# Two transformer blocks in f32 on one core: a new opening, four gate groups as triples, one mask instruction for two, softmax rows scaled on ScalarE

## The chip, the core and the metric

The kernel runs on one core of a Trainium2 chip. The core has TensorE (PE, matrix products into PSUM), VectorE (DVE), ScalarE (ACT), GpSimd (POOL) and SyncE (SP), which here only issues transfers. Each engine runs its own instructions in order and waits for others by semaphores. The metric is the device time of one execution in microseconds; less is better.

## The reference

Two blocks follow each other on x of 256 tokens by 2048 features. What the change touches is in this cut:

```python
c_act = jax.nn.silu(c)
mod = c_act @ w_ada[l] + b_ada[l]                    # 6 x 2048 values: shifts, scales, gates
sh1, sc1, gt1, sh2, sc2, gt2 = jnp.split(mod, 6, axis=-1)
h = modulate(rms_norm(x, g_mix[l]), sh1, sc1)        # h * (1 + sc1) + sh1
z = h @ w_in[l]
(q_sb, k_sb, v_sb, q_ds, k_ds, v_ds, q_ix, k_ix, w_ix, gate_sb, gate_ds) = split_columns(z)
o_sb = stick_breaking_attention(...)                 # strictly causal, 8 heads of 128
o_ds = indexer_sparse_attention(...)                 # top-k keys by an indexer, softmax, 8 heads
merged = (jax.nn.sigmoid(gate_sb) * (o_sb @ w_o_sb[l])
          + jax.nn.sigmoid(gate_ds) * (o_ds @ w_o_dsa[l]))
x = x + gt1[:, None, :] * (merged @ w_out[l])
...
```

After it come a gated feed-forward of width 5632, and the second block: a norm, a mixer with 8 "nsa" heads (two softmaxes each) and 8 "fox" heads (one softmax each), and a second feed-forward.

## The kernel before

**Products.** x lies transposed in SBUF: 16 k-tiles of 128 features by 256 tokens. A weight is cast to a short f32 (`wh`, on ACT, line 298) and its rest is kept beside it (`wl`, weight minus `wh`, on DVE, line 305; the very first `wl` is made on POOL, line 303). Activations are kept as such a pair too (hi and lo). A product of one 128x128 weight tile with one k-tile is made on PE in one of two forms in `mm_f`. As a *triple*: `wh` x hi, `wh` x lo, `wl` x hi, three matmuls of 256 columns into the same 256 columns of PSUM (lines 349 to 351). As a *pair* (`pair=True`): `wh` times hi and lo side by side, 512 columns, and `wl` x hi, 256 columns (lines 343 to 347); the two halves of PSUM are summed at the end by `gather` (lines 454 and 455): a copy of the first half by ACT, then an add of the second by DVE.

**Order of the work.** `items` is a list, written by hand, of weight blocks of 512 KB (`w`), of blocks of the transposed `w_ada` (`ada`), and of calls. SP loads them in this order into ten (later six) raw buffers; a buffer is free again when DVE has read it (`wl`, or the ada reduction). `run` goes through the groups of products and, ahead of each block, has the casts and the `wl` of the blocks up to three ahead issued (`AHEAD`), the cast one step before the `wl` (`LAG`). An ada item is one DVE reduction of 128x1024 (line 313) with the silu of c, spread over all partitions (`cb`); it gives half of a column of `mod`. Attention heads, norms and the like are generators; `tick`, called after every 1.27 us of PE columns, moves each one step on.

**The opening.** SP loads c, the vectors, x in four transfers and then the raw blocks. PE spreads c over the partitions in four matmuls of 512 columns with one row (line 540), ACT makes their silu into `cb` (line 541), and then four squares of x (line 551). DVE adds them in three steps (lines 554 and 555), and four f32 matmuls with ones sum over the partitions (line 558). `first_norm` (line 560), a call behind the second ada item, takes the reciprocal root: one ACT step, the table of Ln and Exp, Ln, Exp, and four POOL steps (567 to 570) into `rb`. Six ada items on, `h_scale(0)` multiplies the first two k-tiles by `rb` on DVE (line 583), two ada items later `first_h` applies `gain` and `mod` (592 to 605), and products begin. The further k-tiles are scaled on POOL by `h_scale`, in six parts of 2, 2, 3, 3, 3 and 3 k-tiles (`KG`); in each part all columns of `w_in` but the gates get their share over the part's k-tiles.

**Behind the parts.** Stick-breaking heads (`sb_head`, line 633) run beside the last part: two multiplies by the mask `strict` of the blocks on the diagonal, in `nk` and again in `a` (lines 649, 650, 663, 664). Then 32 gate tiles in eight groups of four (`ggs`, line 1031, all pairs); the first four groups (gate_sb) run beside the indexer and its top-k search on DVE. The evacuation of a gate tile is `gate_tile` (line 1001). In softmax heads (`ds_head` 851, `nsa_head` 1544, `fox_head` 1626) `softmax` takes the row maximum on DVE and the exponential with its row sum on ACT; DVE takes the reciprocal, and `scale_rows` (line 840) multiplies the two blocks of rows, 128x128 and 128x256, by it on DVE. `transpose_p` (848) needs the result on PE. `rsqrt_of` (line 492) is the reciprocal root used elsewhere: Ln and Exp on ACT and five DVE steps. PSUM holds four buffers `pg` for products and four `pm` (`psm`) for all else and for every second group of the first five parts.

Of the kernel before, what the change touches and what calls it, by code (L numbers as in the profile page):

```python
# [28 lines left out]
LATE_SMALL = (3, 2)  # L29
OFFS = (1, 2, 1.5, 1, 1, 1)  # L30
FS = (0.8, 0.8, 0.8, 0.8, 0.8, 0.8)
FIRSTS = 1
LESS = 2
RL = (0.75, 0.6)
MORE = 12
# [4 lines left out]
LAND = 45  # L40

FILL = (7, 20)
KG = (2, 2, 3, 3, 3, 3)
KG0 = tuple(sum(KG[:j]) for j in range(len(KG)))

# [78 lines left out]
def kernel(ctx: ExitStack, tc: tile.TileContext, t):  # L124
# [40 lines left out]
    def slot(dt=F32):  # L165
        return ring.tile([128, 8, T], dt, name="ring", tag="ring")
# [24 lines left out]
    def psm():  # L191
        return pm.tile([128, 512], F32, name="pm", tag="pm")

    tables = [None]

    def lut(func, **kw):

        if func in (AF.Exp, AF.Ln) and tables[0] != "ln_exp":
            nc.scalar.add_instruction(mybir.InstLoadActFuncSet(
                name=nc.get_next_instruction_name(), act_func_set_id=LN_EXP, engine=mybir.EngineType.Activation,  # L200
                ins=[], outs=[]))
            tables[0] = "ln_exp"
        elif func not in (AF.Exp, AF.Ln):
            tables[0] = func
        nc.scalar.activation(func=func, **kw)  # L205

# [41 lines left out]
    def call_item(fn):  # L248
        items.append(("call", fn))
# [37 lines left out]
    def split(idx, g, ks, off, stage):  # L287

        it, r = items[idx], raw_of[idx]
        k0, n = ks[0], len(ks)  # L290
        if it[0] == "w":
            w = g.width
            src = r[:, k0 - it[2]:k0 - it[2] + n, off:off + w]
            view = lambda x: x[:, :n * w].rearrange("p (k w) -> p k w", w=w)
            if stage == 0:
                hi = view(wp.tile([128, 1024], F32R, name="wh", tag="wh"))
                half_of[idx, g, k0] = hi
                nc.scalar.activation(out=hi, in_=src, func=AF.Copy)  # L298
            else:
                hi, lo = half_of[idx, g, k0], view(wq.tile([128, 1024], F32R, name="wl", tag="wl"))  # L300
                if state["firsts"]:
                    state["firsts"] -= 1
                    nc.gpsimd.tensor_tensor(out=lo, in0=src, in1=hi.bitcast(F32), op=OP.subtract)
                else:
                    nc.vector.tensor_sub(out=lo, in0=src, in1=hi.bitcast(F32))  # L305
                half_of[idx, g, k0] = (hi, lo)
            return
        if stage == 0:
            return

        c, half = ADA[it[1]][0] + it[2] // 2, it[2] % 2
        below = mod[:, c:c + 1] if half else V["b_ada"][:, c:c + 1]
        nc.vector.tensor_tensor_reduce(out=r, in0=r, in1=P["cb"][:, RAW * half:RAW * half + RAW], scale=1.0,  # L313
                                       scalar=below, op0=OP.mult, op1=OP.add, accum_out=mod[:, c:c + 1])
        if half:
            ada_done.add(c)
# [49 lines left out]
            if last:  # L366
                g.evac(b, g.ps[b])

    state = {"load": 0, "split": [0, 0], "raws": 10, "n": 0, "firsts": FIRSTS}
    AHEAD = (3, 3)  # L370
    LAG = 1

# [162 lines left out]
    nc.vector.memset(onec, 1.0)  # L535
    nc.vector.memset(halfc, 1.5)
    nc.vector.memset(invp, 1.0 / 128)
    for u in range(4):
        ps = psm()
        nc.tensor.matmul(ps, ones[0:1, :], P["cb"][0:1, 512 * u:512 * u + 512], start=True, stop=True)  # L540
        lut(out=P["cb"][:, 512 * u:512 * u + 512], in_=ps, func=AF.Silu)
    cdram = dram.tile([1, D], F32, name="cdram")
    nc.scalar.dma_start(out=cdram, in_=P["cb"][0:1, :])

    sqs = []

    def first_squares():
        sqs.extend([slot(), slot()])
        for j in range(4):
            u = slice(4 * (j % 2), 4 * (j % 2) + 4)  # L550
            nc.scalar.activation(out=sqs[j // 2][:, u, :], in_=xt[j // 2][:, u, :], func=AF.Square)
            if j % 2:
                s = sqs[j // 2]
                nc.vector.tensor_add(out=s[:, 0:4, :], in0=s[:, 0:4, :], in1=s[:, 4:8, :])
        nc.vector.tensor_add(out=sqs[0][:, 0:4, :], in0=sqs[0][:, 0:4, :], in1=sqs[1][:, 0:4, :])
        sqs.append(psm())
        for k in range(4):
            nc.tensor.matmul(sqs[2][:, :T], ones, sqs[0][:, k, :], start=(k == 0), stop=(k == 3))

    def first_norm():  # L560
        ss = sqs[2][:, :T]
        m = tmp.tile([128, T], F32, name="mm", tag="mm", bufs=1)
        r0 = tmp.tile([128, T], F32, name="r0", tag="r0", bufs=1)
        nc.scalar.activation(out=m, in_=ss, func=AF.Identity, scale=1.0 / D, bias=epsc)
        lut(out=r0, in_=m, func=AF.Ln)
        lut(out=r0, in_=r0, func=AF.Exp, scale=-0.5)
        nc.gpsimd.tensor_tensor(out=m, in0=m, in1=r0, op=OP.mult)
        nc.gpsimd.tensor_tensor(out=m, in0=m, in1=r0, op=OP.mult)
        nc.gpsimd.tensor_scalar(out=m, in0=m, scalar1=-0.5, scalar2=1.5, op0=OP.mult, op1=OP.add)
        nc.gpsimd.tensor_tensor(out=rb, in0=r0, in1=m, op=OP.mult)  # L570

    def h_segs(j):
        k0, n = KG0[j], KG[j]
# [3 lines left out]
            k0, n = k0 + m, n - m  # L577

    def h_scale(j):
        eng = nc.gpsimd if j else nc.vector  # L580
        for _, b, u, m in h_segs(j):
            x = xt[b][:, u, :]
            eng.tensor_tensor(out=x, in0=x, in1=rb[:, None, :].to_broadcast([128, m, T]), op=OP.mult)
# [49 lines left out]
    def sb_head(h):  # L633
        q, k, v = bufs["q_sb"], bufs["k_sb"], bufs["v_sb"]
        S = psm()
        nc.tensor.matmul(S[:, 0:256], k[:, h, 0:128], q[:, h, :], start=True, stop=True)
        nc.tensor.matmul(S[:, 256:384], k[:, h, 128:256], q[:, h, 128:256], start=True, stop=True)
        yield
        e = P["ax"].tile([128, 384], F32, name="t0", tag="t0")
        l = P["ax"].tile([128, 384], F32, name="t1", tag="t1")  # L640
        lb = P["ax"].tile([128, 384], F32, name="t2", tag="t2")
        nc.scalar.activation(out=e, in_=S[:, :384], func=AF.Abs)
        lut(out=e, in_=e, func=AF.Exp, scale=-1.0)
        lut(out=l, in_=e, func=AF.Ln, bias=onec)
        yield
        nk = P["ax"].tile([128, 384], F32, name="t3", tag="t3")
        nc.vector.scalar_tensor_tensor(out=nk, in0=S[:, :384], scalar=0.0, in1=l, op0=OP.max, op1=OP.add)
        nc.vector.scalar_tensor_tensor(out=lb, in0=S[:, :384], scalar=0.0, in1=l, op0=OP.min, op1=OP.subtract)
        for o in (0, 256):
            nc.vector.tensor_mul(out=nk[:, o:o + 128], in0=nk[:, o:o + 128], in1=C["strict"])  # L650
        yield from wait(W)
        sf = psm()
        nc.tensor.matmul(sf[:, 0:128], C["sufneg"], nk[:, 0:128], start=True, stop=True)
        nc.tensor.matmul(sf[:, 128:256], C["sufneg"], nk[:, 128:256], start=True, stop=False)
        nc.tensor.matmul(sf[:, 128:256], negones, nk[:, 256:384], start=False, stop=True)
        nc.tensor.matmul(sf[:, 256:384], C["sufneg"], nk[:, 256:384], start=True, stop=True)
        yield
        nc.vector.tensor_add(out=lb, in0=sf[:, :384], in1=lb)
        yield
        a = P["ax"].tile([128, 384], F32, name="t4", tag="t4")  # L660
        lut(out=a, in_=lb, func=AF.Exp)
        yield
        for o in (0, 256):
            nc.vector.tensor_mul(out=a[:, o:o + 128], in0=a[:, o:o + 128], in1=C["strict"])
        yield from wait(W)
        yield from av_out(a, [(v, 128 * h)], need_pair("o_sb"), h)

# [171 lines left out]

    def scale_rows(p, r):  # L840
        for b, (o, n) in enumerate(BLK):
            nc.vector.tensor_scalar(out=p[:, o:o + n], in0=p[:, o:o + n], scalar1=r[:, b:b + 1], scalar2=None,  # L842
                                    op0=OP.mult)

    def transpose_p(p):
        PT = psm()
# [98 lines left out]
        gens["h", 0] = None  # L945

    a0 = ada_items(NKG) + ada_items(0)
    items.extend(a0[:2])
    call_item(first_norm)
    items.extend(a0[2:-2])  # L950
    call_item(lambda: h_scale(0))
    items.extend(a0[-2:])
    call_item(first_h)
    extra = [x for a in range(2 * NKG, 2 * NKG + 2) for x in ada_items(a)]
    more = [0] * (NKG - 1) + [MORE]
# [45 lines left out]
    def gate_tile(which, i):  # L1001
        def evac(ps):
            if i % 8 == 0:
                gates[which, i // 8] = slot()
            gather(gates[which, i // 8][:, i % 8, :], ps)
        return evac

    def ds_chain():
# [19 lines left out]
    add_group(k7)  # L1028
    gl = [(t["w_in"], G_SB + 128 * i, gate_tile(0, i)) for i in range(16)]
    gl += [(t["w_in"], G_DS + 128 * i, gate_tile(1, i)) for i in range(16)]  # L1030
    ggs = f_groups(gl, 16, h_act1, idr, pair=True)
    for u, g in enumerate(ggs[:4]):
        if u == 1:
            g.pre = lambda: drain([gens["sb"]])
# [697 lines left out]

    assert not (ada_rest or ada_late or ada_last), (ada_rest, ada_late, ada_last)
    pump_loads(-1)
    first_squares()
    run()
    while active:
        tick()
# [34 lines left out]
```

## Time and profile before

| | |
|---|---|
| time, median of three runs | 2752.37 us (2750.64 to 2767.28) |
| the profiled execution's own time | 2754.54 us |
| its span, first instruction to last | 2751.9 us |
| granted TensorE clock in it, mean | 0.995 |
| instructions | 42323 |

All rows that the prediction uses are from that one execution. Times in rows count from the start of the span. In a row of the timeline the first number is the start, the second the time until the end of the last of the merged instructions; in brackets stands the idle time of the engine before it and what ended it. In a row of a group, `xN` is the count, then come busy time and the mean of one in ns, then idle time before them. A matmul's end is modelled, so its steps are read from the starts. The f32 matmuls (lines 540 and 558) appear as two instructions each.

### The profile page before, as it was taken

What the parts mean: (1) busy time and instruction counts of PE and PEld (TensorE: products, weight loads), DVE (VectorE), ACT (ScalarE), POOL (GpSimd) and SP (SyncE); (2) the same over time, 40 slices, a digit from 0 to 9 for tenths busy, and PEclk for the clock granted to TensorE, in tenths of its full rate; (3) what the DMA queues carried; (4) which work ended last, traced back from release to release, by engine and by line L of the source; (5) the groups of instructions that cost most, each with busy time, mean ns of one, the idle gap of its engine ahead of it and who ended that gap; (6) DMA issues with size and microseconds to landing.
All of it is one profiled execution on the core that took longest, in us unless ns stands there. A gap on an engine that the chain in (4) does not pass through costs nothing. (4 is left out here: it accounts for less than half of the span.)

```text
span 2751.9 us, 42323 instructions
## 1 busy us (share of the span) xinstructions
PE 2671.3 (97%) x15985; PEld 2339.2 (85%) x15985; DVE 1980.9 (72%) x2881; ACT 1364.6 (50%) x2067; POOL 544.9 (20%) x506
## 2 busy tenths in 40 slices
PE   6899999899999999999999999999999999999999
PEld 5788897798987888888888878888888888888888
DVE  7999986998877886556666756677876665566655
ACT  4555563354536555435554535555554454345543
POOL 1655530220612010000111301102222210012210
PEclk9999999999999999999999999999999999999999
DMA  9888767889985886566666675544566666666664
GB/s 324 261 270 265 259 214 201 279 276 331 310 274 157 302 311 194 189 190 188 184 190 200 186 222 150 161 130 146 176 184 192 195 190 191 190 191 191 188 197 143
DMA packets 302045, 591.16 MB, mean 215 GB/s; under 512 B 20997, under 2 KB 60781, under 8 KB 301711
## 3 DMA queue, kind: packets, MB, share of 16 engines
q1 hardware_dynamic: 298214, 583.61, 66.1%
q10 hardware_dynamic: 3626, 4.85, 0.8%
q8 instruction: 125, 2.05, 0.3%
q14 instruction: 80, 0.65, 0.1%
HBM read 582.54 MB, written 5.78 MB: 214 GB/s over the span
## 5 line engine op out<-in xcount | busy, mean ns | idle before, releaser
L347 PE MATMUL pg<-ring,wh 128*128 128x512 f32 x5408 | 1905.0, 394 | 1.1 <-DVE ring L1181 0.9
L305 DVE TENSOR_TENSOR wl<-raw,wh 128x1024 fp32r<-128x1024 f32 (+1 forms) x921 | 1152.0, 1263 | 620.4 <-ACT wh L298 609.9
L346 PE MATMUL pg<-ring,wl 128*128 128x256 f32 x5408 | 1525.4, 282 | 6.5 <-DVE wl L305 4.6
L298 ACT ACTIVATE wh<-raw 128x1024 fp32r<-128x1024 f32 (+2 forms) x922 | 931.5, 1026 | 876.8 <-PE pg L347 652.2
L347 PEld LDWEIGHTS pg<-ring,wh 128*128 128x128 f32 x5408 | 1021.1, 189 | 215.8 <-DVE ring L1181 3.4
L346 PEld LDWEIGHTS pg<-ring,wl 128*128 128x128 f32 x5408 | 1018.8, 188 | 36.1 <-issue 10.3
L481 POOL TENSOR_TENSOR ring<-gy,ring 128x256 fp32r<-128x256 f32 x88 | 110.1, 1262 | 749.5 <-ACT ring L479 749.5
L349 PE MATMUL pg<-ring,wh 128*128 128x256 f32 x652 | 185.6, 285 | 23.6 <-ACT ring L601 13.8
L351 PE MATMUL pg<-ring,wl 128*128 128x256 f32 x652 | 183.9, 282 | 7.4 <-DVE wl L305 7.2
L350 PE MATMUL pg<-ring,wh 128*128 128x256 f32 x652 | 183.4, 281 | 0.0
L343 PE MATMUL pg<-ring,wh 128*128 128x512 f32 x352 | 143.3, 407 | 6.7 <-DVE ring L455 4.7
L349 PEld LDWEIGHTS pg<-ring,wh 128*128 128x128 f32 x652 | 123.6, 190 | 27.6 <-ACT ring L601 14.5
L466 POOL TENSOR_TENSOR ring<-pt,ring 128x256 f32<-128x256 f32 x95 | 110.8, 1174 | 141.5 <-ACT pt L465 141.2
L313 DVE CUSTOM_DVE_ANT_0 raw<-raw,cb,mod 128x1024 f32<-128x1024 f32 x96 | 134.6, 1402 | 1.5 <-DMA raw<-in_w_adaT 1.2
L351 PEld LDWEIGHTS pg<-ring,wl 128*128 128x128 f32 x652 | 123.4, 189 | 10.5 <-DVE wl L305 10.3
L313 DVE CUSTOM_DVE_ANT_0 raw<-raw,cb,vec 128x1024 f32<-128x1024 f32 x96 | 129.0, 1343 | 1.7 <-DMA cb<-cdram 1.6
L350 PEld LDWEIGHTS pg<-ring,wh 128*128 128x128 f32 x652 | 123.5, 189 | 0.8 <-DVE ring L605 0.2
L1247 POOL TENSOR_TENSOR gy<-ga,rb 128x256 f32<-128x256 f32 x44 | 52.5, 1203 | 325.1 <-ACT ga L205 325.1
L344 PE MATMUL pg<-ring,wl 128*128 128x256 f32 x352 | 99.2, 282 | 0.0
L362 PE MATMUL pg<-wh,ring 128*128 128x512 f32 (+3 forms) x236 | 83.5, 354 | 0.0
L364 PE MATMUL pg<-wh,ring 128*128 128x512 f32 (+3 forms) x236 | 79.1, 335 | 0.0
L363 PE MATMUL pg<-wl,ring 128*128 128x512 f32 (+3 forms) x236 | 78.8, 334 | 0.0
(298 smaller groups left out, 2481.3 us busy)
## 6 DMA issues: line engine op xcount, KB each, us to landing
raw<-in_w_in SPq DMA_DIRECT2D x240, 512.0 KB, 4.8
raw<-in_w_adaT SPq DMA_DIRECT2D x192, 512.0 KB, 5.4
raw<-in_w_gate SPq DMA_DIRECT2D x176, 512.0 KB, 4.4
raw<-in_w_up SPq DMA_DIRECT2D x176, 512.0 KB, 3.8
raw<-in_w_down SPq DMA_DIRECT2D x176, 512.0 KB, 4.5
raw<-in_w_out SPq DMA_DIRECT2D x64, 512.0 KB, 5.5
raw<-in_w_o_sb SPq DMA_DIRECT2D x16, 512.0 KB, 5.9
raw<-in_w_o_dsa SPq DMA_DIRECT2D x16, 512.0 KB, 6.4
```

The lines of the kernel that those rows point to most:

```text
L298: nc.scalar.activation(out=hi, in_=src, func=AF.Copy)
L305: nc.vector.tensor_sub(out=lo, in0=src, in1=hi.bitcast(F32))
L313: nc.vector.tensor_tensor_reduce(out=r, in0=r, in1=P["cb"][:, RAW * half:RAW * half + RAW], scale=1.0, scalar=below, op0=OP.mult, op1=OP.a ...
L343: nc.tensor.matmul(g.ps[f], hi[:, fs], both, start=True, stop=False)
L344: nc.tensor.matmul(ps, lo[:, fs], xh, start=False, stop=False)
L346: nc.tensor.matmul(ps, lo[:, fs], xh, start=False, stop=False)
L347: nc.tensor.matmul(g.ps[f], hi[:, fs], both, start=False, stop=stop)
L349: nc.tensor.matmul(ps, hi[:, fs], xh, start=start, stop=False)
L350: nc.tensor.matmul(ps, hi[:, fs], xl, start=False, stop=False)
L351: nc.tensor.matmul(ps, lo[:, fs], xh, start=False, stop=stop)
L466: nc.gpsimd.tensor_tensor(out=y, in0=x, in1=y, op=OP.add)
L481: nc.gpsimd.tensor_tensor(out=lo, in0=src, in1=hi.bitcast(F32), op=OP.subtract)
```

## The change

The opening: a Square of x stands behind each Silu on ACT; DVE adds within each of the two slots, not across them; eight matmuls sum the squares; the table of Ln and Exp is loaded behind the last Square. `first_norm`, now behind the fourth ada item, uses `rsqrt_of` (DVE), issues twelve f32 matmuls of 512 columns whose result nobody reads (`keep_warm`), and calls `h_scale(0)`. The second part's scaling goes from POOL to DVE, and so does the first `wl`. The gate_sb groups become triples and are evacuated by one ACT copy. The two mask multiplies become one instruction over both diagonal blocks. `scale_rows` is done by ACT, as a Copy with a column as its scale.

```diff
-FIRSTS = 1
...
+WARM = 12
...
-    def lut(func, **kw):
-
-        if func in (AF.Exp, AF.Ln) and tables[0] != "ln_exp":
+    def ln_exp():
+        if tables[0] != "ln_exp":
             nc.scalar.add_instruction(mybir.InstLoadActFuncSet(
...
-                if state["firsts"]:
-                    state["firsts"] -= 1
-                    nc.gpsimd.tensor_tensor(out=lo, in0=src, in1=hi.bitcast(F32), op=OP.subtract)
-                else:
-                    nc.vector.tensor_sub(out=lo, in0=src, in1=hi.bitcast(F32))
+                nc.vector.tensor_sub(out=lo, in0=src, in1=hi.bitcast(F32))
...
+    def keep_warm(n):
+
+        ps = psm()
+        for _ in range(n):
+            nc.tensor.matmul(ps, ones, P["cb"][:, :512], start=True, stop=True)
+
+    sqs = [slot(), slot()]
     for u in range(4):
         ps = psm()
         nc.tensor.matmul(ps, ones[0:1, :], P["cb"][0:1, 512 * u:512 * u + 512], start=True, stop=True)
         lut(out=P["cb"][:, 512 * u:512 * u + 512], in_=ps, func=AF.Silu)
+        v = slice(4 * (u % 2), 4 * (u % 2) + 4)
+        nc.scalar.activation(out=sqs[u // 2][:, v, :], in_=xt[u // 2][:, v, :], func=AF.Square)
+        if u % 2:
+            w = sqs[u // 2]
+            nc.vector.tensor_add(out=w[:, 0:4, :], in0=w[:, 0:4, :], in1=w[:, 4:8, :])
     cdram = dram.tile([1, D], F32, name="cdram")
+    sqs.append(psm())
+    for k in range(8):
+        nc.tensor.matmul(sqs[2][:, :T], ones, sqs[k // 4][:, k % 4, :], start=(k == 0), stop=(k == 7))
+    ln_exp()
     nc.scalar.dma_start(out=cdram, in_=P["cb"][0:1, :])
-    sqs = []
-
-    def first_squares():
...
     def first_norm():
...
+        rsqrt_of(rb, sqs[2][:, :T], 1.0 / D, T)
+        keep_warm(WARM)
+        h_scale(0)
...
-        eng = nc.gpsimd if j else nc.vector
+        eng = nc.gpsimd if j > 1 else nc.vector
...
-        for o in (0, 256):
-            nc.vector.tensor_mul(out=nk[:, o:o + 128], in0=nk[:, o:o + 128], in1=C["strict"])
+        ends = lambda x: x.rearrange("p (a b) -> p a b", b=128)[:, 0:3:2, :]
+        strict = C["strict"][:, None, :].to_broadcast([128, 2, 128])
+        nc.vector.tensor_tensor(out=ends(nk), in0=ends(nk), in1=strict, op=OP.mult)
...
-        for o in (0, 256):
-            nc.vector.tensor_mul(out=a[:, o:o + 128], in0=a[:, o:o + 128], in1=C["strict"])
+        nc.vector.tensor_tensor(out=ends(a), in0=ends(a), in1=strict, op=OP.mult)
...
-            nc.vector.tensor_scalar(out=p[:, o:o + n], in0=p[:, o:o + n], scalar1=r[:, b:b + 1], scalar2=None,
-                                    op0=OP.mult)
+            nc.scalar.activation(out=p[:, o:o + n], in_=p[:, o:o + n], func=AF.Copy, scale=r[:, b:b + 1])
...
-    items.extend(a0[:2])
+    items.extend(a0[:4])
     call_item(first_norm)
-    items.extend(a0[2:-2])
-    call_item(lambda: h_scale(0))
-    items.extend(a0[-2:])
+    items.extend(a0[4:])
     call_item(first_h)
...
-            gather(gates[which, i // 8][:, i % 8, :], ps)
+            if which:
+                gather(gates[which, i // 8][:, i % 8, :], ps)
+            else:
+                nc.scalar.activation(out=gates[which, i // 8][:, i % 8, :], in_=ps[:, :T], func=AF.Copy)
...
-    ggs = f_groups(gl, 16, h_act1, idr, pair=True)
+    ggs = f_groups(gl[:16], 16, h_act1, idr) + f_groups(gl[16:], 16, h_act1, idr, pair=True)
...
-    first_squares()
     run()
```

## Rows read from the trace of the kernel before

**Rows 1.** The page's totals: busy time, share of the span and instructions of each engine.

```profile
PE 2671.3 (97%) x15985; PEld 2339.2 (85%) x15985; DVE 1980.9 (72%) x2881; ACT 1364.6 (50%) x2067; POOL 544.9 (20%) x506
```

**Rows 2.** Windows view: stretch, its length, busy us and instructions by engine, PEclk, DMA.

```profile
40.00:50.00 10.00, 10.00 (x83) 9.73 (x82) 10.00 (x17) 6.21 (x10) 0.00 (x0) 1.00 1.00 346
...
60.00:80.00 20.00, 20.00 (x151) 18.81 (x151) 17.67 (x30) 14.21 (x25) 2.22 (x2) 1.00 0.85 270
...
500.00:550.00 50.00, 42.38 (x277) 37.97 (x276) 48.00 (x85) 20.35 (x22) 14.91 (x8) 0.97 0.82 274
```

**Rows 3.** Timeline of the opening: start, us, engine, line, operation.

```profile
2.44 7.16 PE L540 MATMUL pm<-cb,ones 1*128 1x512 f32 x8 [2.44 <-DMA cb<-in_c]
...
3.65 8.42 SPq L268 DMA_DIRECT2D raw<-in_w_adaT  x8
...
10.81 3.89 ACT L551 ACTIVATE ring<-ring 128x1024 f32<-128x1024 f32 x4 [0.58 <-ACT cb L205]
...
17.14 1.28 DVE L313 CUSTOM_DVE_ANT_0 raw<-raw,cb,vec 128x1024 f32<-128x1024 f32 x1
...
17.37 3.75 PE L558 MATMUL pm<-ring,ones 128*128 128x256 f32 x8 [7.77 <-DVE ring L555]
...
21.65 1.28 ACT L199 ACT_TABLE_LOAD   x1
...
27.46 2.34 POOL L303 TENSOR_TENSOR wl<-raw,wh 128x1024 fp32r<-128x1024 f32 x1
27.53 2.81 DVE L583 TENSOR_TENSOR ring<-ring,rb 128x512 f32<-128x512 f32 x1 [2.71 <-POOL rb L570]
...
35.56 1.28 DVE L313 CUSTOM_DVE_ANT_0 raw<-raw,cb,vec 128x1024 f32<-128x1024 f32 x1
35.74 0.42 PE L351 MATMUL pg<-ring,wl 128*128 128x256 f32 x1
...
36.39 0.41 PE L351 MATMUL pg<-ring,wl 128*128 128x256 f32 x1
...
40.54 0.28 PE L351 MATMUL pm<-ring,wl 128*128 128x256 f32 x1
...
42.58 0.28 PE L351 MATMUL pm<-ring,wl 128*128 128x256 f32 x1
```

**Rows 4.** DMA issues in the first 40 us: KB each, median us to landing.

```profile
raw<-in_w_adaT SPq DMA_DIRECT2D x14, 512.0 KB, 8.6
```

**Rows 5.** PE's waits from 80 to 400 us: total us, times, longest.

```profile
PE pg L351 <- DVE wl L305: 7.2, 8, 1.4
```

**Rows 6.** Timeline of PE in the first gate group.

```profile
427.23 0.28 PE L346 MATMUL pg<-ring,wl 128*128 128x256 f32 x1
...
429.31 0.28 PE L346 MATMUL pg<-ring,wl 128*128 128x256 f32 x1
```

**Rows 7.** PE's waits from 480 to 560 us; four adds of `gather` from DVE's timeline.

```profile
PE pg L346 <- DVE wl L305: 3.7, 3, 2.7
...
PE pg L343 <- DVE ring L455: 2.8, 1, 2.8
PE pg L349 <- DVE ring L455: 1.7, 1, 1.7
...
529.34 1.41 DVE L455 TENSOR_TENSOR ring<-pg,ring 128x256 f32<-128x256 f32 x4
```

**Rows 8.** Lines 842, 650 and 1118 (ns min/median/max); ACT's exponentials of softmax rows.

```profile
L842 DVE TENSOR_SCALAR t<-t,st x64: 285/344/1368, 556.9 to 1968.6; 128x128 f32<-128x128 f32 x32, 128x256 f32<-128x256 f32 x32
...
  PE pm L848: 4.8, 4
...
L650 DVE TENSOR_TENSOR t<-t,conA x16: 276/282/837, 356.1 to 420.6; 128x128 f32<-128x128 f32 x16
...
L1118 ACT ACTIVATE ring<-ring,gain x16: 492/495/510, 1486.6 to 1577.2; 128x256 fp32r<-128x256 f32 x16
...
L205 ACT ACTIVATE t<-t,st 128x128 f32<-128x128 f32 x32 | 12.7, 398 | 33.9 <-DVE st L829 25.1 <-DVE st L832 8.6
```

More of the change, by code (lines that the diff above doesn't have):

```diff
@@ L202, in lut @@
             tables[0] = "ln_exp"
-        elif func not in (AF.Exp, AF.Ln):
+    def lut(func, **kw):
+        if func in (AF.Exp, AF.Ln):
+            ln_exp()
+        else:
             tables[0] = func
@@ L367, in mm_t @@
                 g.evac(b, g.ps[b])
-    state = {"load": 0, "split": [0, 0], "raws": 10, "n": 0, "firsts": FIRSTS}
+    state = {"load": 0, "split": [0, 0], "raws": 10, "n": 0}
     AHEAD = (3, 3)
@@ L541 @@
         lut(out=P["cb"][:, 512 * u:512 * u + 512], in_=ps, func=AF.Silu)
+        v = slice(4 * (u % 2), 4 * (u % 2) + 4)
[3 more added lines that the diff above has]
+            nc.vector.tensor_add(out=w[:, 0:4, :], in0=w[:, 0:4, :], in1=w[:, 4:8, :])
     cdram = dram.tile([1, D], F32, name="cdram")
+    sqs.append(psm())
+    for k in range(8):
+        nc.tensor.matmul(sqs[2][:, :T], ones, sqs[k // 4][:, k % 4, :], start=(k == 0), stop=(k == 7))
+    ln_exp()
     nc.scalar.dma_start(out=cdram, in_=P["cb"][0:1, :])
-    sqs = []
-    def first_squares():
[L548 to L558, printed above, removed]
-    def first_norm():
[L561 to L570, printed above, removed]
+    def first_norm():
+        rsqrt_of(rb, sqs[2][:, :T], 1.0 / D, T)
+        keep_warm(WARM)
+        h_scale(0)
     def h_segs(j):
@@ L1004, in evac @@
                 gates[which, i // 8] = slot()
-            gather(gates[which, i // 8][:, i % 8, :], ps)
+            if which:
+                gather(gates[which, i // 8][:, i % 8, :], ps)
+            else:
+                nc.scalar.activation(out=gates[which, i // 8][:, i % 8, :], in_=ps[:, :T], func=AF.Copy)
         return evac
```

## The prediction

> **What bounds the kernel now.** I read the engine totals first. TensorE (PE) is busy 97% of the span, VectorE (DVE) 72%, ScalarE (ACT) 50% [rows 1]: whatever the change does to DVE and ACT counts only where PE waits for them. The windows view says where that is. From 40 us on PE is full, but DVE is full too (10.00 of 10 us at 40 to 50), and over 500 to 550 us DVE has 48.0 of 50 while PE has 42.4 [rows 2]. The timeline of the opening says what happens before: the first triple of products has its third matmul, the one that needs `wl`, at 35.74 us [rows 3], so some 35 us go by with hardly a product. The first triples step by 0.65 us (35.74 to 36.39), the later ones by 0.340 (six of them from 40.54 to 42.58). That is PE at the lower of its two levels, 1.2 GHz, for the first 5 us, and at 2.4 GHz after. Behind the gate groups PE is at work nearly all the time (97% of the span), with products that the change doesn't touch, so I let time that is won in front of them stay won.
>
> **The opening.** Before, the path is: four Silu; four squares in 3.89 us from 10.81; three DVE adds up to 17.1; four f32 matmuls in 3.75 us, so 0.94 each and cold; a table load of 1.28 at 21.65; Ln and Exp; four steps on GpSimd (POOL) until 27.5; the scaling of two k-tiles on DVE, 2.81 because POOL works at the same time; the last two of eight ada reductions; then the first h [rows 3].
> After, step by step. The broadcasts end on PE at 2.44 + 7.16 = 9.6 as before. Each Square (0.97) stands behind its Silu, and the last ends at about 12.2 (it can't end before 9.6 + 0.6 + 0.97 = 11.2). The table load follows there, while nobody waits for it. DVE makes two adds instead of three, the last until 13.5. The sum of squares is eight matmuls instead of four, half of them able to start at the first add: cold, 8 x 0.94 = 7.5 from 10.2, so 17.7 at the latest; I take 16.5, since at the start of the products the higher level came after some 5 us of dense work. DVE meanwhile does four ada reductions at 1.33 each (1.28 and its read), to 18.8. Their data is there: the eight transfers are issued from 3.65 to 12.07 and take 8.6 [rows 3, 4], so they land between 12.3 and 20.3. Then five norm steps of 128x256 on DVE (about 0.35 each, 1.7), the scaling of the first k-tiles (half of a 1.28 pass, 0.65, with POOL now idle), four more ada (5.3), the first h (1.8), and the first `wl`, which POOL made before and DVE makes now (1.2): 18.8 + 1.7 + 0.65 + 5.3 + 1.8 + 1.2 = 29.4. So the third matmul moves from 35.74 to about 29.7, 6.0 earlier.
> The added twelve matmuls wait for nothing but the sum of squares. One of 512 columns takes 7.16 / 4 = 1.79 cold [rows 3], so 0.9 at the higher level: 10.8, and PE is done with them at about 27.3, just ahead of the products, which then step by 0.340 from the first: (40.0 - 35.74) / 0.65 = 6.5 triples x 0.31 = 2.0 won. PE is 8.0 ahead.
> DVE is less far ahead. The next ada reduction starts at 29.4 instead of 35.56 [rows 3], and the second scaling (0.65) comes over from POOL: 5.5. In the first part both engines are full, but DVE has 2.3 us to spare at 60 to 80 [rows 2], so at most 7.8 gets through. From 80 to 400 us PE waits for `wl` again and again (7.2 us in eight waits in the largest group, [rows 5]), so what DVE isn't ahead by is lost. The transfers move with DVE, which frees their buffers. I take 6.5; bounds 2 (a part that starts earlier and then waits for DVE) and 8.0.
>
> **Masks.** Sixteen pairs of 128x128 multiplies (0.282 each, [rows 8]) become sixteen of 2x128. The new form isn't in the trace; the nearest rows are of 128x256, 0.344 [rows 8] and 0.35 (four adds in 1.41, [rows 7]). DVE gets 16 x (0.56 - 0.35) = 3.4 us. This lies at 356 to 430 us, where PE is nearly full, so I take 0.5, between 0 (the elements are the same and one start less is paid, so nothing is lost) and 3.4.
>
> **Gate groups.** Four groups of 64 products go from pairs to triples. A pair steps by 2.08 / 6 = 0.347 (427.23 to 429.31, [rows 6]), a triple by 0.340: the third weight load is covered, and PE saves 256 x 0.0067 = 1.7. The half that holds x-low is now summed in PSUM, so ACT's copy stays and DVE's sixteen adds go (four in 1.41, so 0.35 each and 5.6 us of DVE, [rows 7]). PE waited for such adds 2.8 + 1.7 [rows 7]. What is late next is `wl`: PE already waits 3.7 for it there, and DVE, with the top-k search, is the bound. So in the last two groups the gain is not the whole wait but DVE's time, 8 x 0.35 = 2.8. In the first two, PE-bound, it is 0.85 of PE and about 0.9 of waits. Sum 4.5; bounds 1.7 (the steps alone) and 1.7 + 4.5 + 2.8 = 9.0.
>
> **Softmax rows.** 32 scalings (8 dsa, 16 nsa, 8 fox) of one 128x128 and one 128x256 leave DVE, where the two take 0.28 + 0.34, and come to ACT, where the nearest row, a 128x256 with a column as scale, takes 0.495 and a 128x128 about 0.40 [rows 8]: ACT gets 32 x 0.9 = 28.8 us, DVE loses 20. On DVE these scalings were at times slow (up to 1.37), and PE waited 4.8 us for them in four transposes [rows 8]. ACT has half its time free. But its queue is in order: the scaling now waits for DVE's reciprocal, and the casts to `wh` behind it wait as well, then `wl`, then PE. ACT already stands 33.9 us before 32 exponentials for DVE's row maxima [rows 8]. I take 1.0 of gain; bounds 4.8 gained and 10 lost (a third of 33.9 again).
> The Trainium skill speaks against this edit: "ScalarE: Activation LUTs", section "Rules for kernel authors", wants multiplications on VectorE and not on ScalarE, which is slower per element. The rows agree on the price of one instruction (0.495 against 0.344); by the rule the edit would cost 28.8 - 20 = 8.8 us, if ACT were on the path.
>
> **Sum.** 6.5 + 0.5 + 4.5 + 1.0 = 12.5. The profiled execution took 2754.5 (span 2751.9), so 2742.0; it stood 2.2 above the median of the three runs, 2752.4, so the median goes to about 2740. Its own range, every term moved half-way to its bound, all one way, is 2734 to 2749.
>
> **Rivals.**
> (a) The opening is given back: parts two to six are held by DVE's `wl`, whose total work hardly falls, and the transfers are no earlier when they matter. For it: the waits of [rows 5]. Against: DVE itself starts earlier and had holes (2.7 before the scaling) that go. Opening 2 instead of 6.5: 2744.5.
> (b) Everything at its far end: 8.0 + 3.4 + 9.0 + 4.8 = 25 at most; most of it, 22, is 2730. For it: PE waits for each of the things removed. Against: DVE is full where the adds go.
> (c) Slower: at each of 32 scalings ACT stands for the reciprocal as long as it now stands for the maxima (33.9 / 32 = 1.06) and then works 0.7; the casts behind it are late. Full price 32 x 1.76 = 56 us. It decides once more than 11.5 / 56, a fifth, reaches PE; with a third (19) it ends at 2752.4 - 11.5 + 19 = 2760. For it: DVE idles for `wh` already. Against: `wl` is made three blocks ahead of PE, and ACT is half free.
> (d) The added matmuls don't do what they say: they stay at 1.79 each, 21.5 us from 17.7, and hold PE until 39.2, 3.5 after the old start. The first products then go at the higher level or not; DVE is still ahead, and the opening ends near 0: 2746.5. Against: the products reached the higher level 5 us after they began, on the same full array.
>
> **How the numbers follow.** Chances: forecast 0.55, (a) 0.17, (b) 0.11, (c) 0.11, (d) 0.06. Time 2740, range 2729 to 2753: it takes in (a), (b) and (d), and leaves out most of (c) and the tail of (b). A measurement of this kernel tells about 1% (27.5 us) from no change. Over 1% faster would need all of (b) and more: 0.04. Over 1% slower needs (c) with about 70% of its price: 0.02. Within 1%: 0.94.
>
> **What would show it.** Right: the first triple's third matmul at 28.5 to 31 us; triples at 0.340 from the start; twelve matmuls on PE of about 0.9 that end before it; the first products of part two some 7 us earlier; no PE wait for a DVE add at 500 and 528 us; gate groups 4 to 5 us shorter from first to last; PE's wait before the transposes of softmax rows no longer than 4.8 us in all. Wrong: the added matmuls still running when the first h is ready; the lead at 400 us under 3 us; DVE's idle time for `wh` well above what it was at 553 to 640 and at 1770 to 1970 us, or PE waiting for `wl` behind it.

## The result, and the profile after

The changed kernel takes 2773.19 us (median of 20 runs, 2759.27 to 2779.91); the kernel before, in the runs beside them, 2754.42 (2750.20 to 2769.81). The ratio is 1.0052 (some 14 us; the two medians alone would give 1.0068), with a 95% interval of 1.0039 to 1.0066. Forecast were 2740 and a range of 2729 to 2753: the change was to win 12.5 us, and it loses. The profiled execution took 2764.67 (span 2762.9) against 2754.54 before, so 10.1 longer. Executions fall into two groups some 13 us apart (before: 12 of 20 at 2750 to 2756 and 8 at 2763 to 2770; after: 6 at 2759 to 2767 and 14 at 2772 to 2780), so medians and means move with the share of each group, and below the two traces, both of the shorter group, are compared stretch by stretch.

For that, the making of `wl` of each weight block is counted from the start, and the start of the n-th in one trace is set against the n-th in the trace before. The change of that difference over a stretch is what the stretch won (minus) or lost (plus). Two executions differ in it by 1 to 2 us over a stretch for no reason that I can name.

| stretch (its end in the trace before) | after against before |
|---|---|
| opening, to block 30 (129 us) | -7.0 |
| parts two to six and masks, to block 150 (421 us) | +1.0 |
| gate groups and dsa heads, to block 225 (687 us) | +0.2 |
| nsa and fox heads, block 585 to 660 (1732 to 2016 us) | +17.9 |

Between 687 and 1732 us it moves by another -1.3, to -6.95; at block 660 it is +10.96, and at the end +10.97. So the opening's gain came and stayed for 1700 us, and all that was lost was lost in the nsa and fox heads. The page's totals (engine, busy us and share, instructions) don't tell this; PE is at 97% as in [rows 1]:

```profile
PE 2690.8 (97%) x16273; PEld 2364.7 (86%) x16273; DVE 1954.2 (71%) x2791; ACT 1385.6 (50%) x2130; POOL 536.1 (19%) x500
```

The opening in the timeline of the kernel after (start, us, engine, line, operation, idle time before it), which answers to [rows 3]:

```profile
9.95 5.53 PE L558 MATMUL pm<-ring,ones 128*128 128x256 f32 x16 [0.21 <-DVE ring L554]
...
12.80 1.28 DVE L314 CUSTOM_DVE_ANT_0 raw<-raw,cb,vec 128x1024 f32<-128x1024 f32 x1
...
15.32 10.46 PE L543 MATMUL pm<-cb,ones 128*128 128x512 f32 x24
...
26.88 0.39 PE L350 MATMUL pg<-ring,wh 128*128 128x256 f32 x1 [1.10 <-ACT ring L596]
...
27.54 1.22 DVE L306 TENSOR_TENSOR wl<-raw,wh 128x1024 fp32r<-128x1024 f32 x1
28.68 1.28 DVE L314 CUSTOM_DVE_ANT_0 raw<-raw,cb,vec 128x1024 f32<-128x1024 f32 x1
28.82 0.38 PE L352 MATMUL pg<-ring,wl 128*128 128x256 f32 x1 [1.09 <-DVE wl L306]
29.27 0.28 PE L352 MATMUL pg<-ring,wl 128*128 128x256 f32 x1
...
30.96 0.28 PE L352 MATMUL pg<-ring,wl 128*128 128x256 f32 x1
```

The first triple's third matmul (L352, the one that reads `wl`) starts at 28.82 instead of 35.74, and the triples step by 0.338 from the start (29.27 to 30.96 is five). The next ada reduction follows at 28.68 instead of 35.56. The windows (stretch, length, busy us and instructions of PE, PEld, DVE, ACT, POOL, then granted clock, DMA share, GB/s) say who holds whom after that:

```profile
40.00:50.00 10.00, 10.00 (x66) 8.95 (x64) 10.00 (x16) 6.47 (x10) 0.00 (x0) 1.00 1.03 395
60.00:80.00 20.00, 18.48 (x132) 17.24 (x133) 19.96 (x31) 11.65 (x19) 6.96 (x5) 1.00 0.87 289
```

At 60 to 80 DVE had 2.3 us to spare and PE was full [rows 2]; now DVE is full and PE has 1.5 to spare.

Now the heads, in windows over the same work: the kernel before from 1735 to 2016, cut at 1860,

```profile
1735.00:1860.00 125.00, 122.50 (x716) 104.15 (x715) 88.91 (x210) 69.37 (x140) 15.32 (x10) 0.99 0.46 134
1860.00:2016.00 156.00, 151.29 (x873) 129.79 (x873) 125.08 (x249) 84.75 (x156) 38.44 (x36) 0.99 0.52 166
```

and the kernel after from 1728 to 2027:

```profile
1728.00:1860.00 132.00, 125.71 (x728) 106.26 (x727) 82.53 (x183) 80.09 (x169) 14.82 (x10) 0.99 0.43 129
1860.00:2027.00 167.00, 154.78 (x862) 131.84 (x861) 119.04 (x229) 90.63 (x175) 36.75 (x36) 0.96 0.50 154
```

Of the 18 us, 11.3 are PE's idle time (6.3 + 12.2 against 2.5 + 4.7) and 6.7 are the same products taking longer. ACT gained 17 us of work and DVE lost 12, and neither is near full. So it isn't load; what is it? The waits of the kernel after from 1735 to 2020 us (who <- for whom: total us, times, longest):

```profile
DVE wl L306 <- ACT wh L303: 64.0, 31, 5.0
...
ACT t L210 <- DVE st L827: 14.0, 5, 3.7
ACT t L837 <- DVE st L1633: 12.2, 7, 2.4
ACT t L210 <- DVE st L824: 11.9, 7, 2.1
...
ACT t L837 <- DVE st L1550: 6.9, 6, 1.6
...
DVE t L821 <- POOL t L1628: 5.8, 2, 3.7
...
PE pg L344 <- DVE ring L1130: 5.5, 2, 3.1
...
PE pm L1373 <- ACT wh L303: 3.8, 1, 3.8
...
PE pm L842 <- ACT t L837: 2.1, 2, 1.8
```

The moved scaling is L837. ACT stands before it for DVE's reciprocal (L1550, L1633), in all 21.2 us in 14 places with the 2.1 for L1551. PE hardly waits for the scaled rows themselves (2.1). It waits for what stands behind them: a cast to `wh`, an evacuation L1130. DVE's wait for the casts was there before, but shorter; over 1735 to 2016 us of the kernel before it is

```profile
DVE wl L305 <- ACT wh L298: 52.2, 28, 5.0
```

against 67.0 in the kernel after over the same work (1728 to 2027). One instance, first on ACT's queue,

```profile
1951.51 0.80 ACT L837 ACTIVATE t<-t,st 128x128 f32<-128x128 f32 x2 [1.50 <-DVE st L1633]
...
1953.10 1.04 ACT L303 ACTIVATE wh<-raw 128x1024 fp32r<-128x1024 f32 x1
1955.57 0.40 ACT L837 ACTIVATE t<-t,st 128x128 f32<-128x128 f32 x1 [1.43 <-DVE st L1633]
1955.67 0.33 ACTq L1624 DMA_DIRECT2D cb<-scr  x1
...
1956.49 2.18 ACT L303 ACTIVATE wh<-raw 128x1024 fp32r<-128x1024 f32 x2
```

then on DVE's,

```profile
1954.17 1.22 DVE L306 TENSOR_TENSOR wl<-raw,wh 128x1024 fp32r<-128x1024 f32 x1 [2.70 <-ACT wh L303]
1955.32 0.15 DVE L1633 RECIPROCAL st<-st 128x2 f32<-128x2 f32 x1
...
1960.38 0.29 DVE L821 CUSTOM_DVE_ANT_0 t<-pm,t 128x128 f32<-128x128 f32 x1 [2.08 <-POOL t L1628]
...
1961.80 0.88 DVE L1130 TENSOR_TENSOR ring<-pg,ring 128x256 f32<-128x256 f32 x2
```

and on PE's:

```profile
1959.30 0.40 PE L348 MATMUL pg<-ring,wh 128*128 128x512 f32 x1
1962.82 0.77 PE L344 MATMUL pg<-ring,wh 128*128 128x512 f32 x1 [3.12 <-DVE ring L1130]
...
1963.60 0.41 PE L347 MATMUL pg<-ring,wl 128*128 128x256 f32 x1
...
1964.24 0.41 PE L347 MATMUL pg<-ring,wl 128*128 128x256 f32 x1
```

DVE waits 2.70 us for ACT's cast, makes `wl`, and only then the reciprocal of 0.15. ACT has been waiting for just that, 1.43, with two more casts behind it, and behind the wait too the issue of the next fox head's load of `cb` (L1624 runs on ACT's queue). The load lands late, POOL's add waits for it, DVE's row maximum for POOL, the evacuation L1130 behind that in DVE's order, and PE for the evacuation. Each engine's order holds the other. Then the products step by 0.64 (1963.60 to 1964.24), the lower of PE's two levels, where they stepped by about 0.35: that is the second loss. The granted clock of 0.96 from 1860 on is 8% of 167 us at the lower level, 13.4 us, against 2% or 3.1 before; half of the 10.3 between them, some 5 of the 6.7 by this estimate, is lost that way.

### The profile page after: what moved, and what is told of

The parts are those of the page before. It is cut to its first block, busy times and chain, and to the rows that moved or that the text cites. A ratio compares the mean times of both kernels' runs of the same rounds, so it can differ in the third digit from the quotient of the medians.

```text
span 2762.9 us, 42889 instructions
## 1 busy us (share of the span) xinstructions
PE 2690.8 (97%) x16273; PEld 2364.7 (86%) x16273; DVE 1954.2 (71%) x2791; ACT 1385.6 (50%) x2130; POOL 536.1 (19%) x500
## 4 chain that ended last, share of the span: by engine, by line
PE 76%; DVE 10%; issue 4%; DMA 4%; ACT 3%; POOL 2%; SPq 0%; ACTq 0%; DVEq 0%; POOLq 0%
PE pg L348 39%; PE pg L347 20%; DVE wl L306 4%; DVE raw L314 3%; PE pg L344 2%; PE pg L352 2%; PE pg L350 2%; PE pg L351 2%; DMA raw<-in_w_in 2%; ACT wh L303 2%; PE pg L345 1%; PE pm L680 1%; PE pg L363 1%; PE pg L365 1%; PE pg L364 1%
## 5 line engine op out<-in xcount | busy, mean ns | idle before, releaser
L348 PE MATMUL pg<-ring,wh 128*128 128x512 f32 x5168 | 1819.7, 394 | 1.1 <-DVE ring L1176 0.9
L306 DVE TENSOR_TENSOR wl<-raw,wh 128x1024 fp32r<-128x1024 f32 (+2 forms) x922 | 1150.8, 1260 | 643.3 <-ACT wh L303 639.2
L348 PEld LDWEIGHTS pg<-ring,wh 128*128 128x128 f32 x5168 | 975.3, 189 | 206.8 <-DVE ring L1176 3.3
L352 PE MATMUL pg<-ring,wl 128*128 128x256 f32 x908 | 257.0, 283 | 15.8 <-DVE wl L306 15.7
L350 PE MATMUL pg<-ring,wh 128*128 128x256 f32 x908 | 260.0, 286 | 12.1 <-DVE ring L1047 3.7
L351 PE MATMUL pg<-ring,wh 128*128 128x256 f32 x908 | 256.4, 282 | 0.1
L350 PEld LDWEIGHTS pg<-ring,wh 128*128 128x128 f32 x908 | 173.0, 190 | 20.8 <-issue 4.9
L352 PEld LDWEIGHTS pg<-ring,wl 128*128 128x128 f32 x908 | 172.8, 190 | 20.2 <-DVE wl L306 20.2
L351 PEld LDWEIGHTS pg<-ring,wh 128*128 128x128 f32 x908 | 172.9, 190 | 0.9 <-DVE ring L600 0.3
L344 PE MATMUL pg<-ring,wh 128*128 128x512 f32 x336 | 137.3, 409 | 9.6 <-DVE ring L1130 5.5
```

Source lines behind the costliest of these rows:

```text
L344: nc.tensor.matmul(g.ps[f], hi[:, fs], both, start=True, stop=False)
L348: nc.tensor.matmul(g.ps[f], hi[:, fs], both, start=False, stop=stop)
L350: nc.tensor.matmul(ps, hi[:, fs], xh, start=start, stop=False)
L351: nc.tensor.matmul(ps, hi[:, fs], xl, start=False, stop=False)
L352: nc.tensor.matmul(ps, lo[:, fs], xh, start=False, stop=stop)
```

## The experiments

**Which part loses.** Four kernels take the change apart: the changed kernel with the scalings back on DVE, and the kernel before with one part of the change each.

```diff
 # a_rows_dve (changed kernel)
-nc.scalar.activation(out=p[:, o:o + n], in_=p[:, o:o + n], func=AF.Copy, scale=r[:, b:b + 1])
+nc.vector.tensor_scalar(out=p[:, o:o + n], in0=p[:, o:o + n], scalar1=r[:, b:b + 1], ..., op0=OP.mult)
 # b_rows_act (kernel before): the same line the other way round
 # b_opening: the changed kernel, its gates, masks and rows as before
 # b_gates (kernel before)
+            if which:
                 gather(gates[which, i // 8][:, i % 8, :], ps)
+            else:
+                nc.scalar.activation(out=gates[which, i // 8][:, i % 8, :], in_=ps[:, :T], func=AF.Copy)
...
-    ggs = f_groups(gl, 16, h_act1, idr, pair=True)
+    ggs = f_groups(gl[:16], 16, h_act1, idr) + f_groups(gl[16:], 16, h_act1, idr, pair=True)
```

> The changed kernel with one part undone: the softmax rows are scaled on DVE again. Theory A (the scaling on ACT is what costs: ACT stands for DVE's reciprocal, and the casts behind it are late): the stretch of the nsa and fox heads loses its 18 us, the lead of 6 to 7 us from the opening lasts to the end, 2745 to 2749 where the kernel before takes 2752 to 2754. Theory B (the heads' stretch is longer because everything arrives there 7 us earlier and falls differently against the transfers): little comes back, 2760 to 2775.

> The kernel before with only the softmax rows scaled on ACT. Theory A: slower by 15 to 22 us than the kernel before, nearly all of it between the first nsa head and the last fox head (about 1735 to 2020 us), and next to nothing in the dsa heads (550 to 640 us). Theory B: no difference beyond 3 us.

> The kernel before with only the new opening. If the lead of 7 us at the 30th weight block comes from the opening alone and lasts: faster by 5 to 8 us at the end. If the masks or triples are needed to keep it: less than 4.

> The kernel before with only the first four gate groups as triples. By the prediction: faster by 4.5 (1.7 to 9). By what the trace after shows, a lead that stays at 6 through the gate groups, the step from 0.347 to 0.340 and the adds taken away are given back behind the groups: within 1.5 us of the kernel before.

Measured, with the stretches of the table above, each against the kernel before (12 runs each, b_rows_act 7; the kernel before, in the runs beside these four, has a median of 2762.56):

| run | time us | ratio [95%] | to 30 | 30 to 150 | 150 to 225 | 585 to 660 |
|---|---|---|---|---|---|---|
| a_rows_dve | 2748.41 | 0.9975 [0.9954, 0.9997] | -6.8 | -1.8 | -1.6 | 0.0 |
| b_rows_act | 2771.12 | 1.0072 [1.0043, 1.0101] | +0.2 | -1.5 | +0.5 | +18.0 |
| b_opening | 2754.95 | 0.9986 [0.9967, 1.0006] | -6.1 | -1.5 | -0.2 | +0.4 |
| b_gates | 2753.33 | 0.9994 [0.9971, 1.0018] | +0.4 | -0.5 | -1.1 | -0.9 |

The scalings alone, put into the kernel before, lose what the whole change loses in the heads, 18.0 against 17.9, and taking them out of the changed kernel brings it to 0.0. In b_rows_act about 5 of the 18 are lost by 1903 us, before the first fox scaling (1906), and about 13 behind it. ACT's waits for the reciprocals in b_rows_act from 1735 to 2030 us are those of the kernel after, to the tenth:

```profile
ACT t L842 <- DVE st L1637: 12.2, 7, 2.4
...
ACT t L842 <- DVE st L1554: 6.9, 6, 1.6
```

The interval of b_opening takes in 1, so its 6 us show in the trace and aren't clear of noise in the time.

In the eight dsa heads ACT stands 8.8 us for the reciprocal too, and the stretch loses only 0.2 to 0.5. There DVE waits just 7.6 us for casts (553 to 640 us; 3.3 before), so a late cast may have room; that this is why the standing is free isn't shown.

The gate triples win 1.1 of the 4.5 that I gave them, no more than two executions differ by, and at 490 us, behind the first two groups, 0.1. In those two PE is full, and there the triples of b_gates step by 0.357 (ten from 426.48 to 430.05), not by the 0.340 that was read at 40 us; the pairs that they replace took 0.347 [rows 6]:

```profile
426.48 0.28 PE L351 MATMUL pg<-ring,wl 128*128 128x256 f32 x1
...
430.05 0.28 PE L351 MATMUL pg<-ring,wl 128*128 128x256 f32 x1
```

PE's waits of b_gates from 480 to 560 us, which answer to [rows 7]:

```profile
PE pg L351 <- DVE wl L305: 7.0, 6, 2.5
...
PE pg L349 <- DVE ring L1055: 4.3, 2, 2.3
```

and, in the kernel before, one row more than [rows 7] has:

```profile
PE pg L349 <- DVE ring L1052: 3.1, 2, 2.0
```

The waits for the adds (2.8 and 1.7) are gone. But PE waits 7.0 instead of 3.7 for `wl`, and 4.3 instead of 3.1 for merges (the multiply by the gate, on DVE; L1055, before L1052): 11.3 us in all, and 11.3 before. DVE makes both, is busy for 46.2 of 50 us at 500 to 550 (48.0 before), and is late with the next thing.

**Wait or work.** Two kernels add to the kernel before, in `scale_rows`, one property of the moved scaling each, and leave the scaling on DVE: an ACT instruction of the same size that waits for nothing new, or one of 128x2 that reads the reciprocal. Their results are read by nobody.

```diff
 # b_act_work, per block
+            nc.scalar.activation(out=junk[:, :n], in_=con[:, 128:128 + n], func=AF.Copy, scale=epsc)
 # b_act_wait, per scaling
+        nc.scalar.activation(out=junk, in_=r, func=AF.Copy)
```

> The kernel before, rows still scaled on DVE, with added work on ACT that nobody reads: at each of the 32 scalings two Copies with a column as scale, 128x128 and 128x256, from a constant, which wait for nothing of DVE's. Theory A1 (what costs is ACT standing for DVE's reciprocal): at most 4 us more in the stretch of the nsa and fox heads. Theory A2 (what costs is the 23 us of work itself in ACT's queue): 12 to 18 us more there.

> The kernel before, rows still scaled on DVE, with one Copy of the two reciprocals (128x2) on ACT at each of the 32 scalings: ACT has to stand for DVE's reciprocal as in the changed kernel, and works only some 0.2 us. Theory A1: 10 to 18 us more in the stretch of the nsa and fox heads. Theory A2: at most 4.

Measured (10 and 5 runs; the kernel before beside them has a median of 2752.48): b_act_work 2767.83, ratio 1.0032 [1.0007, 1.0057], +5.9 in the heads; b_act_wait 2779.75, 1.0083 [1.0045, 1.0120], +13.8 in the heads. The line of the small instruction in b_act_wait (ns min/median/max, first and last start; then ACT's idle time before it):

```profile
L845 ACT ACTIVATE junk<-st x32: 187/203/205, 554.9 to 1993.0; 128x2 f32<-128x2 f32 x32
...
  DVE st L1558: 14.1, 15
  DVE st L1640: 12.2, 7
```

24 instructions of 0.2 us, 4.9 us of work whose result goes nowhere, cost 13.8 because of 26.3 us of standing. So most of the loss is the wait. The work at that place counts too: b_act_work, with no wait added, loses 5.9, which lies between what its two theories gave it (at most 4, or 12 to 18).

**The wait taken away.** If the wait does it, the scaling on ACT should be free as soon as it is issued after the reciprocal is there. These versions of the changed kernel issue it two steps of `tick` later: a_rows_late in all heads; a_late_2nd in nsa and fox alone, with dsa on DVE at its old place.

```diff
 # fox_head; nsa_head alike, both p behind the wait; ds_head in a_rows_late alone
+        yield from wait(2)
         scale_rows(p, st[:, 0:2])
-        yield from wait(W)
+        yield from wait(W - 2)
```

> The changed kernel, with the scaling on ACT put two steps of the generators later (so two of the three steps that the heads waited in front of the transposes stand ahead of it). Theory A1: DVE's reciprocal is done when ACT comes to the scaling, the wait and most of the 18 us go, 2743 to 2750. Theory A2: the work is the same, so it stays above 2757. A third outcome: the scaling now comes too late for the transposes, and PE waits there.

> The changed kernel with the dsa rows scaled on DVE and the nsa and fox rows on ACT two steps later. If the wait for the reciprocal is the cost, and the late scaling of the dsa rows is what lost the 8 us in their stretch before: the lead of 8 to 10 us over the kernel before at the 210th weight block, none of it lost in the nsa and fox heads (within 2 us), 2741 to 2746 in its lower level. If ACT's work counts for itself: 5 to 6 us lost there, 2747 to 2752.

Measured: a_rows_late 2766.02, 1.0025 [0.9996, 1.0053] (10 runs; one of them took 4389 us, which I can't explain, and isn't in the ratio; the kernel before beside it 2752.48); a_late_2nd 2749.01, 0.9975 [0.9955, 0.9995] (12 runs; the kernel before 2759.07). In nsa and fox they lose 0.0 and 0.3, with the same 48 instructions on ACT. The line of the scalings in a_late_2nd, with ACT's idle time before them, once 21.2:

```profile
L837 ACT ACTIVATE t<-t,st x48: 384/448/504, 1778.0 to 1974.6; 128x128 f32<-128x128 f32 x24, 128x256 f32<-128x256 f32 x24
...
  DVE st L1637: 1.8, 3
```

But a_rows_late loses 6.6 in block 150 to 225: its lead goes from 7.9 to nothing in the dsa heads, where PE now waits 4.7 us for scaled rows at the transposes, against 0.2 in the kernel after. Two steps later is too late there: with the dsa rows back on DVE (a_late_2nd) the same stretch wins 2.3. The place has to be found for each kind of head.

**The opening's matmuls, and the masks.** Without the twelve matmuls that nobody reads (in b_opening and in a_rows_dve), and the masks alone on the kernel before:

```diff
 # b_opening_cold, a_rows_dve_cold
-        keep_warm(WARM)
 # b_masks: both diagonal blocks of nk, and of a, in one multiply
-        for o in (0, 256):
-            nc.vector.tensor_mul(out=nk[:, o:o + 128], in0=nk[:, o:o + 128], in1=C["strict"])
+        nc.vector.tensor_tensor(out=ends(nk), in0=ends(nk), in1=strict, op=OP.mult)
```

> The new opening alone without the twelve matmuls that nobody reads. By the prediction they are worth 2.0 us: the products start at the same time, 28.8 us, but step by 0.65 for the first 4 to 5 us; at the 30th weight block the lead over the kernel before is 4 to 5 us instead of 6 to 7. If DVE sets the pace of the first part: no difference beyond 0.5 us.

> The changed kernel with the rows on DVE and without the twelve matmuls. If these are worth nothing because DVE sets the pace of the first part: the same lead at every weight block as with them, within 1.5 us, 2741 to 2747 in its lower level. If they are worth the 2 us of the prediction: a lead smaller by 1.5 to 2.5 from the 15th block on.

> The kernel before with only the two mask multiplies as one instruction. One of them over two diagonal blocks takes 0.34 to 0.42 us against 2 x 0.28, so 2 to 3.5 us less of DVE between 356 and 430 us; at the 165th weight block the time moves by 0 to 1 us.

Measured: b_opening_cold 2758.07, 0.9997 [0.9972, 1.0022], lead at block 30 6.6 (10 runs; the kernel before 2752.48); a_rows_dve_cold 2753.53, 0.9987 [0.9962, 1.0012], lead 6.5 (12 runs); b_masks 2765.40, 1.0013 [0.9991, 1.0036], +2.2 in the stretch of the masks, so no gain that shows (8 runs; the kernel before beside both 2759.07). The multiply over two blocks takes 0.416, where two of 128x128 took 0.56:

```profile
L651 DVE TENSOR_TENSOR t<-t,conA x8: 408/416/722, 358.7 to 422.8; 128x256 f32<-128x256 f32 x8
```

The windows of b_opening_cold:

```profile
20.00:30.00 10.00, 2.54 (x9) 2.08 (x10) 9.73 (x18) 4.62 (x6) 0.00 (x0) 0.50 1.05 413
30.00:40.00 10.00, 10.00 (x74) 10.00 (x74) 10.00 (x15) 5.10 (x10) 0.00 (x0) 0.84 1.04 405
...
60.00:80.00 20.00, 19.11 (x139) 17.71 (x139) 19.96 (x30) 12.05 (x20) 8.22 (x6) 1.00 0.85 287
```

The granted clock is 0.50 at 20 to 30 and 0.84 at 30 to 40 (1.00 in b_opening and in the kernel after), and triples step by 0.64 until about 33 us. Yet the lead at block 30 is 6.6, against 6.1 with the matmuls (and 6.5 against 6.8 with the rows on DVE): DVE has 19.96 of 20 us at 60 to 80 in both, and it sets the pace.

## Why the prediction was wrong, point by point

**Opening: right in size, wrong in one reason.** Taken 6.5, measured 7.0 (6.1 alone). The steps held: the sum of squares ends at 15.5 (taken 16.5), the twelve matmuls take 0.87 each (0.9) and end at 25.8 (27.3), the third matmul comes at 28.8 (29.7). But the 2.0 for the higher level was nothing. I had seen that only what DVE is ahead by gets through, and still let 2.3 of DVE's slack pass PE's gain; that slack is what the earlier start uses up. So rival (a) was off, and (d) too: the matmuls did what they say, and it was worth nothing. What counts is DVE: its next ada reduction starts 6.9 earlier (28.68 against 35.56, taken 6.2), near the whole lead. That 6.5 came close with a term in it that is worth nothing is in part luck.

**Masks:** taken 0.5; nothing that shows. The instruction was taken as 0.35 and takes 0.416, so DVE gets 2.3 us instead of 3.4.

**Gate groups:** taken 4.5, measured 1.1, below the bound of 1.7. The step of PE was taken from one short stretch at 40 us and didn't hold: 0.357 against the pair's 0.347 makes 128 triples of the first two groups about 1 us slower (an estimate), where 0.85 was to be won. In the last two groups PE isn't what sets the time. "What is late next is `wl`" was written, and then DVE's 2.8 us were counted as if they came through whole; PE's waits there sum to 11.3 as before.

**Softmax rows: the step that failed.** It took a gain of 1.0 with a bound of 10 lost; it loses 18. The pieces were there: the in-order queue, the casts behind it, 33.9 us of standing for DVE's maxima [rows 8]. What went wrong is the weight put on "ACT has half its time free". An average of half says nothing about a queue that stands 1.5 us in front of a cast that DVE and PE need next. Rival (c) had the mechanism, the place and the price, 56 us at full and a third reaching PE (19); 18 of 56 did, and it had a chance of 0.11. (Its 0.7 of work per scaling should be the 0.9 of the softmax term; that makes the full price 63.) With 18 lost in the place of 1.0 won the sum is -12.5 + 19 = +6.5; the other 4 to 5 us up to the 11 of the trace are mostly the gates and masks, 5.0 forecast and nothing seen in the whole change. The 14 us of the ratio are 3 more than the trace's 11; for these no stretch of the two traces gives a cause.

The Trainium skill ("ScalarE: Activation LUTs", "Rules for kernel authors") wants multiplications on VectorE because it is faster per element (the figure there is for bf16; here the rows are f32). It was right on the edit as made, but not shown by its reason: the work alone at that place cost 5.9, against the 8.8 worked out in the prediction, with nothing taken off DVE, and the same work two steps later, with DVE relieved, cost 0.3; the runs put the larger part, 13.8, on the wait. For that, the Trainium skill ("TensorE: Matmul & The Clock Gate"), section "Architectural detail: the array is 16× 32×32, not 1× 128×128", has the fact that counts: the queues of ScalarE and VectorE are strictly first in, first out. The instance at 1951 to 1963 agrees: two casts and a load's issue, which need nothing of the reciprocal, start only after the scaling.

**Left open:** how much of fox's 13 us goes by the late load of `cb` (POOL waits 44.7 us for it in five places, before 17.7 in three) and how much by the casts. The trace shows both, and no run parts them. In b_act_work POOL waits 36.0 us for these loads and DVE 4.9 us for POOL (6.6 in the kernel after), yet fox loses only about 3 there; that speaks for the load as the smaller part, and doesn't show it. The best versions are a_rows_dve and a_late_2nd, both 0.9975 with intervals below 1, and not told apart.

## What to carry to other kernels

Before a step is moved to an engine that is "half free", look at the place where it will stand: which producer it waits for, and which instructions (casts, evacuations, DMA issues) stand behind it in that queue for others. Where two engines hand work to each other both ways, instructions of 0.2 us that wait can cost more than all the work that is moved (13.8 against 5.9 here); issuing the step a little later, when its operand is there, can make it free, but the place differs by stage. And time won on an engine that isn't the pace (warm products, a saved add) is worth what the engine that is lets through. A product's step is read in the stretch where it is to be used.

## What the runs showed of the hardware that I had not expected

A product can step at two paces at the same granted clock. At 1200 us the pair takes 0.347 in the trace before (six from 1199.87 to 2.08 us later) and 0.354 in that of b_gates (five from 1199.98 to 1.77 later), both with a granted clock of 1.00 over 1100 to 1300 us and PE 200.00 of 200 busy. One trace can hold both: in the kernel after the triple takes 0.338 at 29 to 31 us and 0.357 at 426 (seven from 426.17 to 2.50 later), at a granted clock of 1.00 in both places. The six traces in which the pair takes the slower pace in the first feed-forward spend 10 to 13 us more there than the trace before, as much as the change itself. No run here shows what chooses between the paces.

A gap can cost more than its length. After the 3.1 us at 1959 to 1962 PE runs at its lower level until about 1966.4 (a granted clock of 0.50 at 1963 to 1966). Not every gap does it: behind 2.35 us at 1924 to 1926 the granted clock is 1.00 (1926 to 1934). In the heads such stretches make some 5 of the 18 us by the estimate above, beside 11.3 of idle time.
